# Eight taps of a 31-tap depthwise convolution as fp32 diagonal products on TensorE, in two stages of a two-block network

## The chip, the cores and the metric

The kernel runs on one core of a Trainium2 chip. The metric is the device time of one execution in microseconds (us). A core has five engines that run their own queues in order: TensorE (PE, with its weight loads listed as PEld), VectorE (DVE), ScalarE (ACT), GpSimd (POOL) and SyncE (SP), which here issues the transfers.

## The reference, cut to what matters

Two networks of two layers each run one after the other over 256 tokens of 1024 features. Each layer of the first one has a convolution branch and a recurrence branch, over `x` and over a context `ctx`:

```python
def conformer_conv(u, conv_w, conv_b, cnorm_g, cnorm_b):
    val, gate = jnp.split(u, 2, axis=-1)
    z = val * jax.nn.sigmoid(gate)
    z = dwconv(z, conv_w) + conv_b          # 31 taps per channel, 512 channels
    z = group_norm(z, CONV_GROUPS, cnorm_g, cnorm_b, LN_EPS)
    return jax.nn.silu(z)
...
    yc, s_f, s_b = rwkv_scans(prep_c, s_zero, s_zero, emit=not last)
    yx, _, _ = rwkv_scans(prep_x, s_f, s_b, emit=True)
    mix_x = jnp.concatenate([conformer_conv(ux[..., :CONV_IN], *cv), rwkv_out(yx, prep_x, *post)], axis=-1)
    x = x + gt1 * (mix_x @ w_out[l])
```

All data are fp32. The convolution output at token t is the sum over 31 taps j of `w[j, channel] * z[t + j - 15, channel]`, plus a bias per channel.

## The kernel before

Activations are kept feature-major: 128 channels on the partitions, 256 tokens along the free axis, so 512 convolution channels are four slices f = 0 to 3 of 128 x 256. Large products are made from a high and a low part of each operand (`mm3`, three products); each weight tile of 128 x 1024 (512 KB) is loaded through SP into one of four `raw` slots (L345 to L349) and split on ACT (L341) and DVE (L342).

The program is written in an order of priority, and a planner that simulates the engines (`schedule_with_timeline_sim`) turns it into one in-order queue per engine: of the instructions that it believes ready, the one written earlier goes first, and later ones fill the gaps.

The first network runs four recurrences: context and x of layer 0, context and x of layer 1. The first (`wide(0, ...)`) and the last (`wide(1, ...)`) have a convolution beside them and are the ones touched. In such a stage:

- `rwkv` prepares keys and decays, then `inverse` (L943) inverts 32 x 32 triangles by forward substitution on DVE: 31 steps of a product (L961) and a subtraction (L963), each waiting for the one before. Meanwhile PE runs `reads` (L1013 to L1038) and `values` (L1040 to L1072), whose results DVE masks (L1028, L1064). After it, `chain` (L1074) runs four steps for each of two groups.
- `filler` (L1426) hands out steps between the chain's steps in program order: first `conv_in` (L659), which makes `z` in the tile `x` (four steps, products with `in_wc`, gate on ACT at L669, product on DVE at L670), then `ada_steps` (L478): 32 weight tiles `in_ada`, each read straight from its `raw` slot by two fp32 products of 512 columns; each group of four tiles is copied by ACT (L497) and added to a bias by DVE (L503).
- `conv` (L700), written after the recurrence, makes the 31 taps of each slice. DVE multiplies the middle tap with the bias added (L718) and adds 18 taps with one instruction each (L725) into a tile `T1c`. POOL zeroes its own sum (L719), takes the 12 outer taps, each as a product (L731) and an addition (L732), and adds DVE's sum (L736). The group norm over the result follows (L744 to L762). Its instructions can run as soon as `z` is there, so the planner puts them into the recurrence as fillers.

A third convolution (over x of layer 0, `hold=True`, all 31 taps on POOL) lies beside later work. PSUM tiles of the fillers are two buffers with the tag `pb`, shared by `conv_in` and `ada_steps`.

Of the kernel before, what the change touches and what calls it, by code (L numbers as in the profile page):

```python
# [11 lines left out]
AF = mybir.ActivationFunctionType  # L12
ALU = mybir.AluOpType

P = 128
D = 1024
NF = 8
T = 256
# [16 lines left out]

NLAST = 2, 4

NPOOL, NPOOLE, NPOOLC = (12, 0), (12, 0), (30, 0)
NTAP = 2

QB, QE, QC, EVERY = (2, 3, 4, 5), (2, 3, 4, 5), (1,), 2
# [126 lines left out]
def _layout(a):  # L168
    f = {}
    n = {k: np.asarray(v) for k, v in a.items()}  # L170
# [38 lines left out]
    for l in range(2):  # L209
        f[f"ada{l}"] = n["ada_w"][l].reshape(4, 2, P, 12, 512).transpose(3, 0, 2, 1, 4).reshape(48, P, 1024)  # L210
        w = n["w_in"][l]
# [5 lines left out]
        uc = _up(w[:, :D])  # L217
        f[f"wc{l}"] = (np.stack([uc[:4], uc[4:]], 1).reshape(8, P, D))
        f[f"wo{l}"] = (n["w_out"][l].reshape(NF, P, D))
        lo = np.zeros((P, 2, 1024), np.float32)  # L220
        lo[:64, 0] = n["decay_up"][l].transpose(1, 0, 2).reshape(64, 1024)
        lo[64, 0] = n["decay_b0"][l].reshape(1024)
# [13 lines left out]
        w = n["w_in_2"][l]  # L236
# [17 lines left out]
    "A h 5,P l 5,A h 6,A h 7,D l 6,D l 7").split(",")]  # L254
EVAC = [(e, op, int(f)) for e, op, f in EVAC]
EVAC1 = [x for f in range(8) for x in (("DA"[f // 2 % 2 == 0], "e", f), ("A", "h", f), ("P" if f in (4, 5) else "D", "l", f))]


class Prog:
# [437 lines left out]
            self.split(src, *mix[f])  # L697
        return mix

    def conv(self, l, z, acc, npool, hold=False):  # L700


        nc = self.nc
        o = COLS[f"convw{l}"][0]
        taps = sorted((j for j in range(31) if j != 15), key=lambda j: abs(j - 15))
        nv, na = 30 - npool[0] - npool[1], npool[1]
        parts = [("v", taps[:nv]), ("a", taps[nv : nv + na]), ("p", taps[nv + na :])]

        order = []
        for k, js in parts:  # L710
            order += [((i + 0.5) / len(js), k, j) for i, j in enumerate(js)]
        order.sort()
        zc = [acc[:, f, :] for f in range(4)]
        for f in range(4):
            w = lambda j: self.cols[:, o + 4 * j + f : o + 4 * j + f + 1]
            av = self.T1([P, T]) if nv else None
            if nv:
                nc.vector.tensor_scalar(av, z[:, f, :], w(15), self.col(f"convb{l}", f), ALU.mult, ALU.add)  # L718
                nc.gpsimd.memset(zc[f], 0.0)  # L719
            else:  # L720
                nc.gpsimd.tensor_scalar(zc[f], z[:, f, :], w(15), None, ALU.mult)
            for i, (_, k, j) in enumerate(order):
                d, s = slice(max(0, 15 - j), min(T, T + 15 - j)), slice(max(0, j - 15), min(T, T + j - 15))
                if k == "v":
                    nc.vector.scalar_tensor_tensor(av[:, d], z[:, f, s], w(j), av[:, d], ALU.mult, ALU.add)  # L725
                else:
                    t = self.t(self.pool, [P, T], "tap", bufs=NTAP)
                    if k == "a":
                        nc.scalar.mul(t[:, d], z[:, f, s], w(j))
                    else:  # L730
                        nc.gpsimd.tensor_scalar(t[:, d], z[:, f, s], w(j), None, ALU.mult)  # L731
                    nc.gpsimd.tensor_add(zc[f][:, d], zc[f][:, d], t[:, d])  # L732
                if i % 5 == 4:
                    yield
            if nv:
                nc.gpsimd.tensor_add(zc[f], zc[f], av)  # L736
            else:
                nc.gpsimd.tensor_scalar(zc[f], zc[f], self.col(f"convb{l}", f), None, ALU.add)
# [672 lines left out]
    def first(self):  # L1411
        nc = self.nc
# [3 lines left out]
        drain = lambda g: [None for _ in g]  # L1416
# [4 lines left out]
        fl = lambda t: t.rearrange("p (a b) -> p a b", a=4)  # L1421
        z = lambda: self.t(self.pool, [P, 4, T], "z", bufs=2)

        def wide(l, x, s0, ada, perm, before=None):

            def filler():  # L1426

                steps = itertools.chain(self.conv_in(l, x, fl(self.x[0])), self.ada_steps(l, ada))

                def fill(n=1):  # L1430
                    lane = self.lane
                    self.on("b")
# [32 lines left out]
        zx = z()  # L1465
# [9 lines left out]
        f = self.out(0, self.x, 1, cm)  # L1475
# [3 lines left out]
        self.on("b")  # L1479
        acc = z()  # L1480
        self.go = False
        self.bg = self.conv(0, zx, acc, NPOOLC, True)
# [13 lines left out]
        f = self.out(0, self.x, 0, xm)  # L1496
# [141 lines left out]
```

## Time and profile before

| what | value |
|---|---|
| three timed runs | 2770.84, 2770.74, 2761.48 us (median 2770.74) |
| the profiled execution | 2761.92 us, its span 2760.1 us |
| PE busy | 2615.7 us (95% of the span) |
| DVE busy | 1724.0 us (62%) |
| ACT busy | 1312.7 us (48%) |
| POOL busy | 636.7 us (23%) |
| mean granted TensorE clock | 0.964 |

Busy time is the union of an engine's instruction times. The granted clock is a share of full speed: 1.00 is 2.4 GHz, 0.50 is 1.2 GHz, and a value between them is a mean over a stretch. Times within the execution count from the start of the span. Each fp32 product of PE appears as two records.

### The profile page before, as it was taken

To read this page: it belongs to the slowest core of one execution; us is meant where nothing else is said; L and a number is where in the kernel's file an instruction comes from. 1 tells how busy PE (TensorE), PEld (TensorE's weight loads), DVE (VectorE), ACT (ScalarE), POOL (GpSimd) and SP (SyncE) were. 2 spreads that over 40 slices of the span, in tenths; PEclk is the share of its full clock that TensorE was granted. 3 is DMA by queue.
4 is the path that set the end of the run, shared out by engine and by line. 5 is a ranking of instruction groups with operands and counts; after the bars stand their busy time and mean duration, and the time that the engine had idled before them with its cause. 6 is when DMAs were issued, how large, how long until landed. Compare 5 with 4: busy or idle time off the path is not lost.

```text
span 2760.1 us, 53694 instructions
## 1 busy us (share of the span) xinstructions
PE 2615.7 (95%) x22398; PEld 2279.0 (83%) x22398; DVE 1724.0 (62%) x2739; ACT 1312.7 (48%) x1985; POOL 636.7 (23%) x625
## 2 busy tenths in 40 slices
PE   7889989999889998889899899999999999999998
PEld 4858867888678897856799899889899898889897
DVE  3895778645577555995555655666655655756655
ACT  5514654434564346423544544644544544644543
POOL 0397999900130001384100000010000000100000
PEclk9998999999899999998999999999999999999999
DMA  7363425334323354252455555524555554425653
GB/s 252 108 207 130 144 80 187 126 129 163 114 77 116 130 183 145 100 202 93 145 184 186 195 185 188 190 77 160 184 186 182 190 184 175 164 85 183 209 187 115
DMA packets 118768, 430.71 MB, mean 156 GB/s; under 512 B 13174, under 2 KB 13686, under 8 KB 118524
## 3 DMA queue, kind: packets, MB, share of 16 engines
q1 hardware_dynamic: 118524, 427.28, 44.9%
q8 instruction: 175, 2.87, 0.4%
q14 instruction: 69, 0.57, 0.1%
HBM read 425.13 MB, written 2.10 MB: 155 GB/s over the span
## 4 chain that ended last, share of the span: by engine, by line
PE 80%; DVE 11%; ACT 4%; issue 2%; DMA 2%; POOL 1%; SPq 0%; ACTq 0%; DVEq 0%; POOLq 0%
PE pb L333 33%; PE acc L333 25%; PE ps L333 20%; DVE wl L342 3%; DVE T1c L725 1%; DVE S L963 1%; DMA raw<-in_ada 1%; DVE T L961 1%; ACT wh L341 1%; PE acc L438 1%; DVE acc L619 0%; DVE x L620 0%; DMA raw<-in_wr 0%; DVE S L849 0%; ACT L384 0%
## 5 line engine op out<-in xcount | busy, mean ns | idle before, releaser
L342 DVE TENSOR_TENSOR wl<-raw,wh 128x1024 fp32r<-128x1024 f32 (+1 forms) x654 | 811.8, 1245 | 608.6 <-ACT wh L341 383.8
L341 ACT CAST wh<-raw 128x1024 fp32r<-128x1024 f32 (+1 forms) x654 | 682.0, 1046 | 887.9 <-PE pb L333 349.7
L333 PE MATMUL pb<-xf,wh 128*128 128x256 f32 (+1 forms) x2560 | 489.2, 289 | 14.6 <-DVE T1b L588 5.1
L333 PE MATMUL pb<-S,wh 128*128 128x256 f32 x2560 | 490.5, 288 | 3.5 <-DVE S L630 1.7
L333 PEld LDWEIGHTS pb<-xf,wh 128*128 128x128 f32 (+1 forms) x2560 | 411.3, 195 | 29.2 <-DVE T1b L588 8.9
L333 PEld LDWEIGHTS pb<-S,wh 128*128 128x128 f32 x2560 | 407.0, 191 | 20.3 <-issue 11.2
L333 PE MATMUL ps<-S,wh 128*128 128x256 f32 x2048 | 390.0, 287 | 1.3 <-ACT S L460 0.9
L333 PE MATMUL pb<-xf,wl 128*128 128x256 f32 (+1 forms) x1280 | 372.0, 291 | 9.2 <-DVE wl L342 9.2
L365 POOL TENSOR_TENSOR wl<-raw,wh 128x1024 fp32r<-128x1024 f32 x22 | 52.7, 2407 | 1400.8 <-ACT wh L364 964.9
L333 PE MATMUL pb<-S,wl 128*128 128x256 f32 x1280 | 366.5, 286 | 1.8 <-DVE wl L342 1.8
L333 PEld LDWEIGHTS ps<-S,wh 128*128 128x128 f32 x2048 | 325.9, 191 | 11.2 <-issue 4.0
L333 PE MATMUL ps<-S,wl 128*128 128x256 f32 x1024 | 292.9, 286 | 0.0
L333 PEld LDWEIGHTS pb<-xf,wl 128*128 128x128 f32 (+1 forms) x1280 | 249.1, 195 | 17.1 <-DVE wl L342 12.0
L333 PEld LDWEIGHTS pb<-S,wl 128*128 128x128 f32 x1280 | 245.0, 191 | 5.2 <-issue 2.3
L333 PE MATMUL acc<-wh,T 128*128 128x512 f32 x704 | 206.3, 393 | 0.0
L333 PEld LDWEIGHTS ps<-S,wl 128*128 128x128 f32 x1024 | 195.8, 191 | 2.5 <-issue 1.5
L333 PE MATMUL acc<-wh,T1b 128*128 128x512 f32 x528 | 158.3, 398 | 3.5 <-ACT T1b L341 3.5
L731 POOL TENSOR_SCALAR tap<-z,cols 128x255 f32<-128x255 f32 (+14 forms) x120 | 148.3, 1245 | 0.0
L333 PEld LDWEIGHTS acc<-wh,T 128*128 128x128 f32 x704 | 127.0, 189 | 23.6
L731 POOL TENSOR_SCALAR tap<-x,cols 128x246 f32<-128x246 f32 (+5 forms) x96 | 110.7, 1163 | 46.1 <-DVE x L670 46.1
L333 PEld LDWEIGHTS acc<-wh,T1b 128*128 128x128 f32 x528 | 95.2, 190 | 22.4 <-ACT T1b L341 4.4
L333 PE MATMUL acc<-wl,T 128*128 128x512 f32 x352 | 113.1, 395 | 0.0
(444 smaller groups left out, 3907.6 us busy)
## 6 DMA issues: line engine op xcount, KB each, us to landing
raw<-in_fu SPq DMA_DIRECT2D x132, 512.0 KB, 3.2
raw<-in_ada SPq DMA_DIRECT2D x96, 512.0 KB, 4.2
raw<-in_pu SPq DMA_DIRECT2D x88, 512.0 KB, 4.2
raw<-in_qu SPq DMA_DIRECT2D x88, 512.0 KB, 3.3
raw<-in_fd SPq DMA_DIRECT2D x66, 512.0 KB, 3.2
raw<-in_wr SPq DMA_DIRECT2D x51, 512.0 KB, 3.5
raw<-in_pd SPq DMA_DIRECT2D x44, 512.0 KB, 4.0
raw<-in_qd SPq DMA_DIRECT2D x44, 512.0 KB, 3.3
```

The lines of the kernel that those rows point to most:

```text
L333: return self.nc.tensor.matmul(out, lhsT, rhs, start=start, stop=stop, **kw)
L341: self.nc.scalar.copy(hi, src)
L342: self.nc.vector.tensor_sub(lo, src, hi.bitcast(F32))
L365: self.nc.gpsimd.tensor_sub(lo, r, hi.bitcast(F32))
L438: nc.tensor.transpose(pt[f // 2][:, f % 2, b, :], yb[b][:, f * P : f * P + P], self.cst("ident"))
L725: nc.vector.scalar_tensor_tensor(av[:, d], z[:, f, s], w(j), av[:, d], ALU.mult, ALU.add)
L731: nc.gpsimd.tensor_scalar(t[:, d], z[:, f, s], w(j), None, ALU.mult)
L961: nc.vector.tensor_mul(tv, tj[:, k + 1 : 32, k : k + 1].broadcast_to([P, m, k + 1]), X[:, k : k + 1, 0 : k + 1].broadcast_to([P, m, k + 1]))
L963: nc.vector.tensor_sub(X[:, k + 1 : 32, 0 : k + 1], X[:, k + 1 : 32, 0 : k + 1], tv)
```

## The change

A new step `conv_first` makes the eight middle taps (15, 14, 16, 13, 17, 12, 18, 11) of each slice on PE: for each tap an fp32 product of a 128 x 128 diagonal matrix with the shifted slice of `z`, all eight summed in one PSUM tile. ACT copies the sum to `acc` and adds the bias. The diagonals are made on the host (`cd0`, `cd1`: four tiles of 512 KB for each layer) and loaded through the same `raw` slots. `conv_first` stands in the filler between `conv_in` and `ada_steps`. In `conv`, DVE zeroes its sum with a memset and adds 12 taps, and POOL takes 11 taps and adds them to the `acc` that ACT wrote. The held convolution keeps its 31 taps on POOL, with the bias now in its first instruction.

```diff
-NPOOL, NPOOLE, NPOOLC = (12, 0), (12, 0), (30, 0)
+TAPS = sorted(range(31), key=lambda j: abs(j - 15))
+NTENS, NPOOL = 8, 11
...
+    def conv_first(self, l, z, acc):
+        for f in range(4):
+            r = self.raw(f"cd{l}", f)
+            pc = self.ps((P, T))
+            for i, j in enumerate(TAPS[:NTENS]):
+                d, s = tap(j)
+                self.mm(pc[:, d], r[:, i * P : i * P + P], z[:, f, s], i == 0, i == NTENS - 1)
+            self.nc.scalar.activation(acc[:, f, :], pc, AF.Identity, bias=self.col(f"convb{l}", f))
+            yield
...
-                nc.vector.tensor_scalar(av, z[:, f, :], w(15), self.col(f"convb{l}", f), ALU.mult, ALU.add)
-                nc.gpsimd.memset(zc[f], 0.0)
+                av = self.T1([P, T])
+                nc.vector.memset(av, 0.0)
+                for j in TAPS[NTENS : 31 - n]:
+                    d, s = tap(j)
                     nc.vector.scalar_tensor_tensor(av[:, d], z[:, f, s], w(j), av[:, d], ALU.mult, ALU.add)
...
-                steps = itertools.chain(self.conv_in(l, x, fl(self.x[0])), self.ada_steps(l, ada))
+                steps = itertools.chain(self.conv_in(l, x, fl(self.x[0])),
+                                        self.conv_first(l, fl(self.x[0]), fl(self.x[1])), self.ada_steps(l, ada))
...
-            drain(self.conv(l, fl(self.x[0]), fl(self.x[1]), (NPOOL, NPOOLE)[l]))
+            drain(self.conv(l, fl(self.x[0]), fl(self.x[1])))
```

## Rows read from the trace of the kernel before

**Rows 1.** Page, engines: busy time, share of the span, instructions of PE.

```profile
PE 2615.7 (95%) x22398; PEld 2279.0 (83%) x22398; DVE 1724.0 (62%) x2739; ACT 1312.7 (48%) x1985; POOL 636.7 (23%) x625
```

**Rows 2.** Chain that ended last, shares by line, in four stretches (139-163, 163-206, 1160-1197, 1197-1262).

```profile
by line: DVE T1c L725 49.6%; DVE wl L342 16.3%; DVE T L961 9.6%; DVE S L963 6.7%; DVE S L1028 6.5%; issue 4.5%; DVE x L670 2.8%; PE acc L333 2.7%; DVE T1c L718 2.7%
...
by line: PE pb L333 52.3%; PE acc L333 21.5%; DMA raw<-in_ada 15.2%; PE acc L1051 4.9%; PE acc L1034 3.8%; ACT T2b L497 2.8%; issue 0.6%; ACTq L497 0.1%
...
by line: DVE T1c L725 41.7%; DVE wl L342 17.0%; DVE S L963 11.5%; DVE T L961 9.7%; DVE S L1028 7.7%; DVE T1c L718 4.9%; DVE x L670 3.6%; issue 3.0%; PE acc L1034 1.3%
...
by line: PE pb L333 45.2%; PE acc L333 30.4%; DMA raw<-in_wo 9.9%; PE ps L333 7.3%; PE acc L1051 3.2%; ACT T2b L497 2.7%; PE acc L1034 2.6%; issue 0.5%; ACTq L497 0.1%
```

**Rows 3.** Busy by stretch, first stage: PE, PEld, DVE, ACT, POOL; clock, DMA, GB/s.

```profile
130.00:206.00 76.00, 67.10 (x657) 44.22 (x660) 73.39 (x156) 16.76 (x29) 68.69 (x65) 0.93 0.57 196
206.00:230.00 24.00, 24.00 (x393) 16.80 (x392) 12.30 (x22) 10.15 (x14) 23.51 (x29) 0.64 0.47 173
230.00:300.00 70.00, 69.03 (x852) 56.31 (x851) 41.80 (x79) 34.22 (x59) 48.20 (x52) 1.00 0.30 101
```

**Rows 4.** Busy by stretch, last stage, the same columns.

```profile
1160.00:1233.00 73.00, 63.96 (x633) 42.32 (x635) 72.03 (x153) 15.18 (x27) 63.32 (x63) 0.95 0.56 196
1233.00:1262.00 29.00, 28.63 (x549) 21.77 (x548) 16.45 (x30) 12.78 (x19) 28.37 (x35) 0.82 0.52 176
```

**Rows 5.** The first row of rows 3 in two parts, the same columns.

```profile
139.00:163.00 24.00, 17.15 (x192) 14.21 (x192) 24.00 (x44) 3.47 (x6) 23.61 (x23) 0.93 0.28 98
163.00:206.00 43.00, 41.26 (x380) 21.73 (x378) 40.39 (x97) 9.83 (x18) 37.53 (x36) 0.92 0.78 267
```

**Rows 6.** DVE by line, 130 to 206: busy us, mean ns, idle before.

```profile
L725 DVE SCALAR_TENSOR_TENSOR T1c<-x,cols,T1c 128x254 f32<-128x254 f32 (+8 forms) x72 | 42.1, 618 | 0.0
...
L718 DVE TENSOR_SCALAR T1c<-x,cols 128x256 f32<-128x256 f32 x4 | 1.8, 440 | 0.0
```

**Rows 7.** Line 725 over the whole span: durations min/median/max in ns.

```profile
L725 DVE SCALAR_TENSOR_TENSOR T1c<-x,cols,T1c x144: 456/476/960, 132.9 to 1230.9; 128x255 f32<-128x255 f32 x16, 128x254 f32<-128x254 f32 x16, 128x253 f32<-128x253 f32 x16, 128x252 f32<-128x252 f32 x16
```

**Rows 8.** PE in order of time (start, us): two successive fp32 products of 256 columns.

```profile
1289.80 0.60 PE L333 MATMUL acc<-x,const 128*128 128x256 f32 x2
1290.23 0.59 PE L333 MATMUL acc<-rks,const 128*128 128x256 f32 x2
```

**Rows 9.** Other groups of that shape over the span: busy us, mean ns of a record.

```profile
L333 PE MATMUL ps<-wa,S 128*128 128x256 f32 x40 | 10.6, 403 | 0.0
...
L333 PE MATMUL ps<-z,const 128*128 128x256 f32 x8 | 4.9, 715 | 0.5 <-DVE z L751 0.5
```

**Rows 10.** PE in order of time, instructions before which it waited.

```profile
141.25 0.39 PE L333 MATMUL pb<-xf,wl 128*128 128x256 f32 x1 [1.37 <-DVE wl L342]
...
153.61 0.38 PE L333 MATMUL pb<-xf,wl 128*128 128x256 f32 x1 [1.98 <-DVE wl L342]
```

**Rows 11.** SP in order of time: issues of loads in the first stage.

```profile
135.94 79.76 SPq L348 DMA_DIRECT2D raw<-in_ada  x32
224.67 8.21 SPq L348 DMA_DIRECT2D raw<-in_wc  x6
```

**Rows 12.** POOL in order of time: its first and last convolution work.

```profile
131.30 1.89 POOL L731 TENSOR_SCALAR tap<-x,cols 128x246 f32<-128x246 f32 x2 [23.33 <-DVE x L670]
...
1265.44 0.78 POOL L736 TENSOR_TENSOR x<-x,T1c 128x256 f32<-128x256 f32 x1
```

**Rows 13.** POOL by line, 130 to 206: busy us, mean ns, idle before.

```profile
L731 POOL TENSOR_SCALAR tap<-x,cols 128x246 f32<-128x246 f32 (+5 forms) x32 | 41.0, 1291 | 23.3 <-DVE x L670 23.3
L732 POOL TENSOR_TENSOR x<-x,tap 128x246 f32<-128x246 f32 (+5 forms) x31 | 26.1, 841 | 1.1
```

**Rows 14.** DVE in order of time: first reader of the finished convolution, last stage.

```profile
1288.69 0.42 DVE L751 TENSOR_TENSOR x<-x,acc 128x256 f32<-128x256 f32 x1 [0.87 <-PE acc L333]
```

**Rows 15.** ACT in order of time: an eviction of 128x256 from PSUM.

```profile
128.82 0.38 ACT L669 ACTIVATE T1b<-pb 128x256 f32<-128x256 f32 x1
```

More of the change, by code (lines that the diff above doesn't have):

```diff
@@ L219, in _layout @@
         f[f"wo{l}"] = (n["w_out"][l].reshape(NF, P, D))
+        cw, cd = n["conv_w"][l].reshape(31, 4, P), np.zeros((4, P, NTENS, P), np.float32)
+        for i in range(NTENS):
+            for p in range(4):
+                cd[p, np.arange(P), i, np.arange(P)] = cw[TAPS[i], p]
+        f[f"cd{l}"] = cd.reshape(4, P, NTENS * P)
         lo = np.zeros((P, 2, 1024), np.float32)
@@ L256, with tap @@
 EVAC1 = [x for f in range(8) for x in (("DA"[f // 2 % 2 == 0], "e", f), ("A", "h", f), ("P" if f in (4, 5) else "D", "l", f))]
+def tap(j):
+    return slice(max(0, 15 - j), min(T, T + 15 - j)), slice(max(0, j - 15), min(T, T + j - 15))
 class Prog:
@@ L698, in mixed_in, with conv @@
         return mix
-    def conv(self, l, z, acc, npool, hold=False):
+    def conv_first(self, l, z, acc):
[7 more added lines that the diff above has]
+            yield
+    def conv(self, l, z, acc, hold=False):
         nc = self.nc
         o = COLS[f"convw{l}"][0]
[L705 to L712, printed above, removed]
+        n = 31 if hold else NPOOL
         zc = [acc[:, f, :] for f in range(4)]
@@ L715, in conv @@
             w = lambda j: self.cols[:, o + 4 * j + f : o + 4 * j + f + 1]
-            av = self.T1([P, T]) if nv else None
-            if nv:
-                nc.vector.tensor_scalar(av, z[:, f, :], w(15), self.col(f"convb{l}", f), ALU.mult, ALU.add)
-                nc.gpsimd.memset(zc[f], 0.0)
-            else:
[L721 to L724, printed above, removed]
+            if hold:
+                nc.gpsimd.tensor_scalar(zc[f], z[:, f, :], w(15), self.col(f"convb{l}", f), ALU.mult, ALU.add)
+            else:
+                av = self.T1([P, T])
+                nc.vector.memset(av, 0.0)
+                for j in TAPS[NTENS : 31 - n]:
+                    d, s = tap(j)
                     nc.vector.scalar_tensor_tensor(av[:, d], z[:, f, s], w(j), av[:, d], ALU.mult, ALU.add)
[L726 to L732, printed above, removed]
+            for i, j in enumerate(TAPS[1:] if hold else TAPS[31 - n :]):
+                d, s = tap(j)
+                t = self.t(self.pool, [P, T], "tap", bufs=NTAP)
+                nc.gpsimd.tensor_scalar(t[:, d], z[:, f, s], w(j), None, ALU.mult)
+                nc.gpsimd.tensor_add(zc[f][:, d], zc[f][:, d], t[:, d])
                 if i % 5 == 4:
                     yield
-            if nv:
+            if not hold:
                 nc.gpsimd.tensor_add(zc[f], zc[f], av)
-            else:
-                nc.gpsimd.tensor_scalar(zc[f], zc[f], self.col(f"convb{l}", f), None, ALU.add)
             yield
@@ L1481, in first @@
         self.go = False
-        self.bg = self.conv(0, zx, acc, NPOOLC, True)
+        self.bg = self.conv(0, zx, acc, True)
         self.mods, self.every = self.ada_steps(1, QC), EVERY
```

## Prediction

> **What bounds the kernel now.** I read the page's engine totals first: PE is busy for 2615.7 us of 2760.1 [rows 1], so 144.4 us of PE idle time is all that the kernel has, anywhere. Work taken from another engine is worth only what it lets PE stop waiting; work given to PE costs its full length except where it lands in that idle time, or lets PE run at its higher clock for longer.
>
> Then I read the chain that ended last, in the two stages that are edited. Each has two parts. Early in the inversion the chain lies on DVE: from 139 to 163 the taps of L725 hold 49.6% of it (11.9 us), and from 1160 to 1197 41.7% (15.4 us) [rows 2]. Later, from 163 to 206 and from 1197 to 1262, it lies on PE: the pb and acc products are 74% and 76% of it, and no tap stands on it [rows 2]. So the taps are costly in the first part and free in the second.
>
> Third, the busy time by stretch. From 130 to 206 DVE is busy 73.39 of 76.00 us, but PE also 67.10, at a mean clock of 0.93 [rows 3]. So PE is idle for 8.9 us. Of that 6.85 lie between 139 and 163 and 1.74 between 163 and 206 [rows 5]. In the last stage PE is idle for 9.04 us of the 73 from 1160 to 1233 [rows 4]. After the inversion PE has no room left: 24.00 of 24.00 and 69.03 of 70.00 in the first stage [rows 3], 28.63 of 29.00 in the last [rows 4].
>
> The clock is a second reserve. It has two levels, 1.2 and 2.4 GHz. A mean of 0.93 over 76 us means 10.6 us at the lower one, and half of that, 5.3 us, is what it cost [rows 3]. In the last stage 0.95 over 73 us gives 7.3 us and 3.7 us [rows 4]. The fall comes where PE has waited for DVE: 1.37 us at 141 and 1.98 us at 153 [rows 10].
>
> **The change part by part.**
>
> *Products added to PE.* Each stage gets 4 slices x 8 taps = 32 fp32 products, of 252 to 256 columns. Successive products of this shape start 0.43 us apart (1289.80 and 1290.23 [rows 8]). 32 x 0.43 = 13.8 us a stage, 27.5 us for both. The upper bound for the usual clock is the product of `ps<-wa,S`: 40 records are 20 products in 10.6 us, 0.53 us each [rows 9], 17 us a stage. At the low clock it would be 1.22 us (8 records, 4 products, 4.9 us [rows 9]), 39 us if all 32 met it. I take 0.43, because these are back to back in one PSUM tile like the pair of rows 8.
>
> *What of this PE would have idled through.* A product of slice f can start when z[f] is there (the first at 131.3, when POOL starts on it [rows 12]), when its diagonals have landed, and when one of two pb buffers is free. The loads queue on SP behind those of `in_wc`, in the place where the 32 of `in_ada` begin at 135.94 [rows 11]. So from about 140 on some products can lie in the 6.85 us of idle time between 139 and 163. Bounds: 0 (if the planner's simulation sees no gap there, or the buffers are held by `conv_in`) and all 8.9 us. I take 5.0 us, a little over half, since the idle time is in the right place and the buffers only partly.
>
> *Clock.* If PE waits less before 160, part of the 5.3 and 3.7 us comes back. Bounds 0 and 5.3; I take 1.5 us a stage, since the small 32 x 32 products and the remaining waits stay as they are.
>
> *Taps removed from DVE.* Six of 18 per slice, 24 a stage, at 42.1 us / 72 = 0.585 us each [rows 6]: 14.0 us. The middle tap of L718 (0.44 us [rows 6]) becomes a memset of the same size, which I put between 0 and that price. DVE falls from 73.4 to about 59 us in the stretch and ceases to be the fuller engine. The instructions of L725 take 476 ns in the median and up to 960 [rows 7]; the long ones lie where POOL works on taps too. The Trainium skill ("SBUF — State Buffer", section "SBUF: two separate sides") says that a DVE instruction with two SBUF inputs and a GpSimd instruction that reads SBUF lock each other out for a whole instruction. By that rule the taps removed should be counted at the free price, 24 x 0.476 = 11.4 us, and the remainder is waiting that other DVE work would inherit. Either way this relief is no term of the sum: it is the means by which PE's idle time shrinks, counted above.
>
> *POOL.* One tap of 12 per slice goes: 4 x (1.291 + 0.841) = 8.5 us less [rows 13], and four memsets. But its additions now wait for the first eviction of PE's sum instead of a memset done long before. In the last stage POOL ends at 1266.2 [rows 12] and the first reader of the finished slice, the group norm, comes at 1288.69 [rows 14]: 22 us of cover. A later start of 15 us less 8.5 us of work stays under it: 0. The cover is gone once the start is over 31 us late, and each further microsecond would then count.
>
> *ACT.* Four evictions a stage at 0.38 us [rows 15], 1.5 us, on an engine that is busy for 16.76 us of 76 [rows 3]: 0.
>
> *Transfers.* Four loads of 512 KB a stage, ahead of the 32 of `in_ada` on SP and in the same four slots. The 32 take 79.76 us, 2.5 us each [rows 11], so four in turn would push the `in_ada` stream by 10 us. Between 139 and 163 the transfers fill only 0.28 of the DMA engines' time, from 163 to 206 0.78 [rows 5], so the loads themselves find room; the push is the slots held until z[f] exists. In the first stage the next loads, `in_wc` at 224.67, come right behind the stream [rows 11] and PE needs them soon after. I take 0, because PE then has its own 13.8 us of work in place of `in_ada`'s, and keep 10 us as the upper bound for the first stage. In the last stage nothing is late.
>
> *The held convolution* loses four POOL instructions of at most 1.3 us [rows 13] out of a POOL run that PE does not wait for in the edited stages: 0.
>
> *Sum.* Per stage 13.8 - 5.0 - 1.5 = +7.3 us; two stages +14.6. Some of the first half of the stage may run earlier because DVE's queue is shorter, so I round down to +13. Against the profiled execution, 2761.9 us, that is 2775. The timed runs show two values, 2761.5 and twice 2770.8; the profiled one is at the lower, the median, 2770.7, at the upper. On the median the forecast is 2784 us.
>
> **The rivals.**
>
> *No change: PE's reserves take it all.* Idle 8.9 + 9.0 and clock 5.3 + 3.7 are 26.9 us, against 27.5 of new work. For it: with DVE relieved, the waits for wl in rows 10 should nearly vanish. Against: the planner fills every gap that it sees on DVE with taps as long as there are any, so the early part stays dense until they run out. Time: -8 to +4 us, 2763 to 2775.
>
> *Faster: the inversion is the true end and PE's fill moves behind it.* DVE's 24 taps less, 14 us a stage, bring the inversion's end from 206 towards 192, and the filler products of `in_ada` that are still to do run in the stretch after it, where PE's clock is 0.64 [rows 3] because it only runs small products. If dense work kept the clock up there, up to 24 x 0.36 = 8.6 us would come back in the first stage and 29 x 0.18 = 5.2 us in the last [rows 3, 4]. The Trainium skill ("TensorE: Matmul & The Clock Gate", section "Part 1: The HAM clock gate (the "warmup" mystery)") has the clock follow how busy the array has been, which speaks for it. With that and all of the idle time the change comes to 27.5 - 26.9 - 13.8 = -13 us, and down to -20 if the shorter DVE queue also brings later waits down. It decides from the point where PE, with its new products but with part of the filler left for later, reaches the inversion's end in the 59 us that DVE then needs. Time: 2750 to 2757.
>
> *Much slower: a late end.* The `in_ada` stream is pushed by its 10 us in the first stage with PE waiting for `in_wc`, or POOL ends past its cover, or the products run at 0.53 us or partly at the low clock (+6 to +15). Time: +25 to +40 us, 2796 to 2811. For it: the two pb buffers are held by `conv_in` nearly throughout the early part, which would put all 32 products behind 163, where PE has 1.74 us of room [rows 5].
>
> *That the change does not do what it says*: the planner could leave the taps on the chain as dense as now. That is the upper half of the forecast.
>
> **How the numbers follow.** Forecast (+4 to +24 us): 0.52. No change: 0.16. Faster: 0.18. Late end: 0.14. A change of 0.5% (13.9 us) is about what a measurement of this kernel can tell from none. Half of the forecast lies above that: slower 0.26 + 0.14 = 0.40; within 0.5% 0.26 + 0.16 = 0.42; faster 0.18. The range must hold 0.8: the forecast and no change are 0.68; I add most of the late end, up to +33 us, and the nearer end of the faster case, down to -17 us: 2754 to 2804. The forecast's own range is 2775 to 2795.
>
> **What would show it.** Right: 64 products with `in_cd` at about 0.43 us, PE busy up by 24 to 30 us, its idle time between 139 and 163 (and 1160 to 1197) down by several us, L725 at 96 records, and the chain that ended last on PE instead of L725. DVE then has idle time late in the inversion. Wrong in the sum: PE's busy time rising by much less than 27 us, which would be the clock; or the whole of the last stage ending earlier than now. Wrong in the cover: POOL's last addition after the group norm's other centring steps, or PE waiting on `in_wc` loads after the first stage.

## The result, and the profile after

The changed kernel takes 2807.04 us (median of five runs, 2803.8 to 2814.22) against 2770.74 us for the kernel before beside it: ratio 1.0145, 95% interval 1.0124 to 1.0165. It is slower, by 36 us between the medians. The forecast was 2784 us with a range up to 2804. Runs more than 1.5% above the fastest of the same kernel are left out of all comparisons below; there is one, in an experiment.

The profiled execution took 2804.08 us, its span is 2802.3, 42.2 longer than that of before. The engine line of its page, to be read against [rows 1]:

```profile
PE 2657.2 (95%) x22526; PEld 2319.7 (83%) x22526; DVE 1699.3 (61%) x2691; ACT 1317.8 (47%) x1996; POOL 585.0 (21%) x597
```

PE has 41.5 us more busy time and 128 more records, DVE has 24.7 us less, POOL 51.7 us less. PE is idle for 145.1 us, against 144.4: none of its idle time was saved in sum.

Where the time came in is read from the two stages. A fixed piece of work bounds each: from SP's first load of `in_wc` to the first of `in_fu` behind it for the first stage, from the first load of the last context's `in_wr` to the `in_fu` behind it for the last. The busy time by stretch (PE, PEld, DVE, ACT, POOL; granted clock, DMA share, GB/s), before:

```profile
94.29:358.78 264.49, 249.00 (x2879) 198.09 (x2869) 198.49 (x381) 118.16 (x204) 200.60 (x207) 0.94 0.45 155
1046.45:1322.14 275.69, 245.96 (x2913) 187.84 (x2912) 207.01 (x395) 117.44 (x204) 128.17 (x138) 0.93 0.38 131
```

and after:

```profile
96.35:387.80 291.45, 270.27 (x2945) 219.19 (x2935) 183.95 (x353) 125.13 (x212) 168.35 (x190) 0.89 0.42 148
1074.83:1364.38 289.55, 266.63 (x2975) 208.65 (x2974) 191.41 (x370) 117.97 (x208) 105.98 (x126) 0.91 0.38 132
```

The first stage is 27.0 us longer, the last 13.9. Each length can be split into three: PE idle (length less busy time), clock loss (one minus the granted clock, times the length: what the stretch would be shorter at full clock, if all of it went by the clock), and the rest, which is called work at full clock. Added over ten equal parts of each stage, since the clock has only two digits, this gives for the change: first stage idle +5.7, clock loss +15.8, work +5.5; last stage idle -6.8, clock loss +8.8, work +11.9. The split is good to some 6 us (a stage in which nothing is changed shows shifts of that size between its parts, below). It puts too much into the clock loss: the products alone are 14.5 us a stage (below), and the work term shows +5.5 and +11.9. A group of eight 64 x 64 records takes 0.68 us at 1.00 (187.89 in the kernel before) and 1.11 at 0.50 (210.74 in the changed one), 1.6 times and not twice. The lengths are no better than some 6 us either: two stages in which nothing is changed moved by 0.7 and 2.1, two kernels with the same first stage took 282.6 and 276.9 us for it, and the 688 us between the two stages, where only the held convolution's bias is changed, are 8.4 us shorter to 12.0 longer than before in the fifteen profiles.

The first stage in finer stretches, for [rows 3] and [rows 5]:

```profile
139.00:163.00 24.00, 24.00 (x274) 22.14 (x273) 24.00 (x57) 5.17 (x9) 4.55 (x5) 1.00 0.32 110
163.00:206.00 43.00, 33.42 (x349) 24.35 (x348) 31.26 (x58) 9.91 (x15) 42.06 (x52) 0.65 0.29 98
206.00:230.00 24.00, 24.00 (x353) 17.08 (x352) 6.04 (x15) 7.02 (x15) 23.53 (x31) 0.70 0.30 106
230.00:300.00 70.00, 67.04 (x769) 45.12 (x767) 28.47 (x62) 24.07 (x46) 8.11 (x11) 0.95 0.60 213
```

From 139 to 163 PE no longer idles at all, where it idled 6.85 us. From 163 to 206 it idles 9.6 us instead of 1.7, and its clock is 0.65 instead of 0.92. Transfers fill 0.29 of the DMA engines' time there instead of 0.78: the stream of `in_ada` stands still. PE in order of time around 176, with the wait ahead of an instruction in brackets:

```profile
172.14 0.68 PE L345 MATMUL acc<-S,S 64*64 64x64 f32 x8
172.75 1.06 PE L345 MATMUL pb<-raw,csil 128*32 128x512 f32 x6
180.65 1.60 PE L345 MATMUL acc<-S,S 64*64 64x64 f32 x16 [6.84 <-DVE T L1074]
```

and DVE, which it waited for (L971 and L973 are the inversion's steps, L739 the taps):

```profile
175.60 0.67 DVE L739 SCALAR_TENSOR_TENSOR T1c<-x,cols,T1c 128x246 f32<-128x246 f32 x1
...
179.59 0.40 DVE L971 TENSOR_TENSOR T<-S,S 128x87 f32<-128x87 f32 x1
180.02 0.25 DVE L973 TENSOR_TENSOR S<-S,T 128x87 f32<-128x87 f32 x1
180.18 0.41 DVE L1074 TENSOR_TENSOR T<-acc,const 64x256 f32<-64x256 f32 x1
...
181.38 0.58 DVE L973 TENSOR_TENSOR S<-S,T 128x31 f32<-128x31 f32 x1
```

The inversion on DVE ends at 182.0, where before it ended at 204.5. But the mask product T of `values`, on which the next PE instruction waits, has been queued behind almost all of it. Behind that wait PE is at 0.50 until about 220. Up to 188.5 it runs four products of `in_ada` there, and from then to 218 none, but mostly 64 x 64 and 32 x 32 products. SP's issues in the first stage, for [rows 11]:

```profile
137.77 13.09 SPq L360 DMA_DIRECT2D raw<-in_cd  x4
157.74 80.55 SPq L360 DMA_DIRECT2D raw<-in_ada  x20
...
240.35 20.18 SPq L360 DMA_DIRECT2D raw<-in_ada  x12
264.06 5.87 SPq L360 DMA_DIRECT2D raw<-in_wc  x5
```

`in_ada` begins 21.8 us later, and `in_wc` 39.4 us later. In PE's queue only 10 of the 64 products of `in_ada` now stand ahead of the inversion's last product, in either stage; before it was 56.

The products themselves, and the taps left, over the span:

```profile
L345 PE MATMUL pb<-x,raw 128*128 128x255 f32 (+4 forms) x128 | 29.0, 380 | 0.0
...
L739 DVE SCALAR_TENSOR_TENSOR T1c<-x,cols,T1c x96: 459/472/925, 134.2 to 1225.0; 128x251 f32<-128x251 f32 x16, 128x250 f32<-128x250 f32 x16, 128x249 f32<-128x249 f32 x16, 128x248 f32<-128x248 f32 x16
```

128 records are 64 products in 29.0 us of busy time, 0.45 us each.

The last stage begins 28.4 us later than before (1074.83 against 1046.45). Its first row below, for [rows 4], ends with PE at 0.96, and the 57 us behind it are at 0.60:

```profile
1160.00:1233.00 73.00, 64.87 (x740) 57.24 (x738) 70.00 (x151) 24.03 (x42) 30.36 (x35) 0.96 0.37 131
1233.00:1290.00 57.00, 55.22 (x811) 44.30 (x810) 23.43 (x48) 15.31 (x26) 47.82 (x61) 0.60 0.17 58
```

In the kernel before, the same part of the stage, 28.4 us earlier, was at 0.91:

```profile
1204.62:1261.62 57.00, 55.76 (x820) 35.82 (x820) 43.48 (x93) 18.30 (x28) 53.11 (x59) 0.91 0.64 221
```

### The profile page after: what moved, and what is told of

It reads as the page before. It is cut to its first block, busy times and chain, and to the rows that moved or that the text cites. A ratio compares the mean times of both kernels' runs of the same rounds, so it can differ in the third digit from the quotient of the medians.

```text
span 2802.3 us, 53922 instructions
## 1 busy us (share of the span) xinstructions
PE 2657.2 (95%) x22526; PEld 2319.7 (83%) x22526; DVE 1699.3 (61%) x2691; ACT 1317.8 (47%) x1996; POOL 585.0 (21%) x597
## 4 chain that ended last, share of the span: by engine, by line
PE 79%; DVE 12%; ACT 4%; DMA 2%; issue 2%; POOL 1%; SPq 0%; DVEq 0%; ACTq 0%; POOLq 0%
PE pb L345 32%; PE acc L345 26%; PE ps L345 20%; DVE wl L354 2%; DVE T1c L739 2%; DMA raw<-in_ada 1%; DVE T L971 1%; DVE S L973 1%; ACT wh L353 1%; PE acc L450 1%; POOL tap L743 0%; DVE S L860 0%; DVE tDb L531 0%; DVE acc L631 0%; ACT L396 0%
## 5 line engine op out<-in xcount | busy, mean ns | idle before, releaser
L345 PEld LDWEIGHTS acc<-wh,T1b 128*128 128x128 f32 x528 | 95.8, 191 | 23.5 <-ACT T1b L353 4.4
L744 POOL TENSOR_TENSOR z<-z,tap 128x255 f32<-128x255 f32 (+14 forms) x120 | 105.3, 878 | 4.0
```

The costliest lines, as they stand in the source:

```text
L345: return self.nc.tensor.matmul(out, lhsT, rhs, start=start, stop=stop, **kw)
```

## The experiments

Each difference is between medians of runs on one chip, with the 95% interval of the ratio; different rows can come from different chips. "First" and "last" are the lengths of the two stages against before in the profiled execution, bounded as above; they do not add up to the difference, which is of other runs and has the time outside the stages in it.

| kernel | against before, us | ratio | first | last |
|---|---|---|---|---|
| changed kernel | +36.3 | 1.0124-1.0165 | +27.0 | +13.9 |
| in_ada held back, nothing else | +49.6 | 1.0167-1.0193 | +29.1 | +25.2 |
| taps out, no products | +14.1 | 1.0041-1.0069 | +2.2 | +14.4 |
| products beside all taps | +43.0 | 1.0141-1.0168 | +29.5 | +25.6 |
| the same, products late | +23.5 | 1.0072-1.0104 | +17.4 | +15.4 |
| in_ada urgent | +45.4 | 1.0152-1.0184 | +24.7 | +20.8 |
| no loads | +30.7 | 1.0094-1.0128 | +12.5 | +18.8 |
| in_ada urgent, no loads | +40.3 | 1.0104-1.0178 | +29.6 | +29.1 |
| T first | +37.6 | 1.0121-1.0155 | +25.6 | +18.3 |
| T first, in_ada urgent | +44.6 | 1.0138-1.0185 | +31.5 | +8.5 |
| T first, in_ada urgent, no loads | +18.5 | 1.0043-1.0079 | +11.6 | +14.9 |
| VectorE keeps 18 taps | +33.6 | 1.0099-1.0140 | +26.0 | +20.1 |
| products behind in_ada | +56.3 | 1.0183-1.0221 | +18.1 | +46.3 |
| the same, first stage only | +10.1 | 1.0030-1.0063 | +12.4 | -2.1 |
| last stage only | +13.5 | 1.0035-1.0064 | -0.7 | +19.6 |

**Is the displaced filler enough by itself?** The kernel before, with PE's products of `in_ada` held behind the inversion:

```diff
-self.conv_in(l, x, fl(self.x[0])), self.ada_steps(l, ada)
+self.conv_in(l, x, fl(self.x[0])), self.held(3, self.ada_steps(l, ada))
...
+with self.tc.issue_after(self.lastinv.ins) if i >= n else contextlib.nullcontext():
```

> The kernel before, all taps on VectorE and GpSimd, no diagonals. One edit: in both stages the products with in_ada from the fourth step on are ordered on TensorE behind the last 32 x 32 product of the inversion, so 12 of 64 run before it instead of 56 (10 in the changed kernel). Theory D (the displaced in_ada products cost what the sum did not hold: TensorE then has only small products during the inversion, at 1.2 GHz and with waits): +10 to +20 us against before, mean granted clock down from 0.964 to about 0.958. Theory W (the unexplained 14 us belong to the diagonal products or their loads themselves): 0, within 4 us.

Measured +49.6 us, with no work added: more than the whole change costs, and two and a half times the top of what the theory allowed. PE idles 15.2 us more in the first stage and 10.3 in the last, and the clock loss rises by 15.5 and 21.9. The loads of `in_ada` wait as well, since its products hold the slots (0.05 of the DMA engines' time from 173 to 206). So the order of the filler is a term of the size of the result. The share that I had given it, in proportion to 14 us, was far too small.

**Fewer taps alone, and products alone.** In the first, `conv_first` is taken out of the changed kernel; in the second, it is added to the kernel before.

```diff
-self.conv_first(l, fl(self.x[0]), fl(self.x[1])), self.ada_steps(l, ada)
+self.ada_steps(l, ada)
```

> The changed kernel without the diagonal products, their loads and their evictions: the eight middle taps and the bias of the two convolutions are left out of the computation, so what is timed is the relief of VectorE and GpSimd alone. 40 and 32 of the 64 products of in_ada run before the inversion's end (56 before). The prediction's own steps (10 us of idle time and 3 us of clock come back): -13 us against before. Theory D: relief and displacement nearly cancel, -6 to +6 us. Theory W (TensorE never gains from fewer taps, nothing is lost either): 0, within 3 us.

```diff
-self.conv_in(l, x, fl(self.x[0])), self.ada_steps(l, ada)
+self.conv_in(l, x, fl(self.x[0])), self.conv_first(l, fl(self.x[0]), None), self.ada_steps(l, ada)
```

> The kernel before with all its taps, and in addition the 64 diagonal products, their loads and evictions (to a tile that nothing reads): the added work alone. 24 and 32 of the 64 products of in_ada run before the inversion's end (56 before). The prediction's product term: +27.5 us, less what lands in idle time, so +18 to +28. Theory D: 27.5 plus 32 + 24 of the 92 displaced products at 14.5 us for all, +33 to +40. Theory W: the products carry the whole loss, +42 within 4 us.

Relief alone costs 14.1 us where the prediction's steps gave -13 us and theory D allowed +6 at most: nearly all of it in the last stage, where 32 of 64 products of `in_ada` are left ahead of the inversion's end, and it is clock loss there (+15.8). That the missing 24 products are the cause is argued from this, not shown. Products alone cost 43.0 us. That is theory W's number (42 within 4) and above theory D's, and within the intervals as much as the whole change: by the medians the relief pays back 6.7 us.

**Is it the products, or where they stand?** The products beside all taps, ordered behind the inversion's last product:

```diff
-self.conv_first(l, fl(self.x[0]), None), self.ada_steps(l, ada)
+self.ada_steps(l, ada), self.held(0, self.conv_first(l, fl(self.x[0]), None))
```

> The kernel before with all its taps, and the 64 diagonal products, their loads and evictions in addition (evicted to a tile that nothing reads), as in the run with the products beside all taps; one edit more: the products are traced after the steps of in_ada and ordered on TensorE behind the last 32 x 32 product of the inversion, so 56 of 64 products of in_ada run before the inversion's end, as before. Theory P (it is the place of the products, ahead of in_ada's and of the value products, that costs the 15 us beyond their own 27.5): +14 to +30 us against before, with the stretch up to the inversion's end as before, and less than 27.5 where the products lift the clock behind the inversion. Theory W (the 15 us belong to the products wherever they stand): +38 to +46.

Measured +23.5: 19.5 us less than the same products ahead of `in_ada`, and less than their own length (64 x 0.45 = 28.8 us, by the rows above). In the first stage the clock loss is that of before (+0.1) and the work +14.6. This settles that the loss beyond the products' own length belongs to their place, on PE and, with their loads, on SP. The last stage still has +10.4 of clock loss there, which stays unexplained.

**Putting the filler back.** In the changed kernel the steps of `in_ada` get a higher priority.

```diff
-self.ada_steps(l, ada)
+self.at(-1000, self.ada_steps(l, ada))
```

> The changed kernel with one edit: the steps of in_ada get a higher priority in the planner, so that 40 (first stage) and 56 (last stage) of their 64 products run before the inversion ends, instead of 10 and 10; taps, diagonals and their loads as changed. Theory D: the time falls by 8 to 15 us against the changed kernel, to +27 to +34 us against before; the last stage, where all 56 are back, gives back most of its half. Theory W: as the changed kernel, +42 within 5 us.

Measured +45.4: a miss for theory D. It is theory W's number (42 within 5), but the run above with the products late speaks against its cause. The filler is back in PE's queue, and the clock still falls. The stretch from 173 to 206, in the columns used above, in the kernel before:

```profile
173.00:206.00 33.00, 31.93 (x312) 17.43 (x316) 30.39 (x71) 7.14 (x14) 32.18 (x30) 0.95 0.77 261
```

in the changed kernel:

```profile
173.00:206.00 33.00, 24.18 (x295) 17.66 (x290) 21.26 (x39) 7.04 (x10) 32.30 (x42) 0.55 0.25 84
```

and in this one:

```profile
173.00:206.00 33.00, 26.54 (x252) 15.61 (x254) 18.87 (x36) 8.01 (x11) 32.29 (x41) 0.57 0.37 125
```

PE's wait for T is still there (its view of waits: us in total, times, longest), and so are the diagonals' loads ahead of `in_ada` on SP.

```profile
PE acc L352 <- DVE T L1081: 6.5, 1, 6.5
```

**Without the loads.** The identity in SBUF takes the diagonals' place in the changed kernel, first alone, then with the filler urgent as well.

```diff
-r = self.raw(f"cd{l}", f)
+r = self.cst("ident")
```

> The changed kernel without the eight loads of diagonals: the stationary operand of all 64 products is the identity that is in SBUF already, so the weights of the eight middle taps are left out of the computation. Planner's order of in_ada 10 and 14 of 64 before the inversion's end. Theory P (order on TensorE): as the changed kernel, +35 to +45 us against before. Theory L (the loads hold the four slots and SyncE's queue ahead of in_ada's, which starts 20 us late): in_ada's first load back near 136 us and +20 to +30.

> The changed kernel with both suspects of the first stage taken away: no loads of diagonals (the identity stands in their place, so the weights of the eight middle taps are left out of the computation) and the steps of in_ada at a higher priority in the planner. 56 and 48 of the 64 products of in_ada run before the inversion's end (56 and 56 before). Theory P + L (order on TensorE and the place of the loads on SyncE are the whole of the first stage's loss beyond the products): the first stage costs 11 to 16 us instead of 26, of which half clock at most 4; the whole +22 to +34 us against before. If a third cause is in the first stage (the wait on VectorE's T alone lets the clock fall for 35 us): the first stage stays at 20 or more, the whole at +38 or more.

Without loads: +30.7, between the two theories. `in_ada` starts at 137.6 us, and the first stage costs 12.5 us instead of 27.0, so about half of that stage's cost comes with the loads; the last stage gains nothing (+18.8), and the whole only 5.6 us by the medians. What goes is not the fall of the clock from 173 to 206, which is as deep as in the changed kernel, behind a wait of 6.0 us for T and with the same 10 products of `in_ada` ahead:

```profile
173.00:206.00 33.00, 27.00 (x382) 21.21 (x375) 23.02 (x41) 9.86 (x15) 32.29 (x40) 0.59 0.22 77
```

It is what follows: the clock is at 1.00 from 215 to the end of the stage, where the changed kernel is at 0.50 until 220 and falls again between 270 and 280 and between 330 and 340. The clock loss is +4.0 instead of +15.8, the idle time -1.6 instead of +5.7, the work +10.1 instead of +5.5.

With the filler urgent as well: +40.3, in five runs spread from 2785 to 2824 us, the profiled one the slowest. In that execution the third cause is there: PE waits 7.0 us for T, and the clock from 173 to 206 is 0.53.

**Taking the wait for T away.** In the changed kernel the inversion's last seven steps are ordered behind the first T on DVE:

```diff
-nc.vector.tensor_mul(tv, ...)
-nc.vector.tensor_sub(X[...], X[...], tv)
+with self.tc.issue_after(self.firstT.ins) if k0 is not None and k >= k0 else contextlib.nullcontext():
+    nc.vector.tensor_mul(tv, ...)
+    nc.vector.tensor_sub(X[...], X[...], tv)
```

> The changed kernel with one edit on VectorE: the last seven steps of the inversion's elimination are ordered behind the first two mask products T of the value products, on which TensorE waited 6.8 us with its clock falling to 1.2 GHz for the next 40 us. TensorE's order stays nearly that of the changed kernel (16 instead of 10 products of in_ada ahead of the inversion's end), and so do the diagonals, their loads and all work. Theory S (that one wait lets the clock fall, and the small products behind it keep it low): the wait falls under 2 us, the clock stays at 2.4 GHz for most of 173 to 206, and the first stage costs 12 to 18 us instead of 26; the whole +22 to +34 us against before. Theory O (the order of TensorE's work alone does it, with small products and no in_ada between): the wait goes, but the clock still falls before 190 us and the first stage stays at 22 or more; the whole +36 to +46.

The longest wait for T falls to 2.2 us, and the time is +37.6 us: theory S falls, and the time lies in theory O's range. The clock holds longer, but is at 0.50 from 188 on, in a stretch without a product of `in_ada` (183.5 to 221). It falls in the second of two waits, of 1.7 and 2.2 us, so the run does not tell the missing products from the waits. Then both edits together, with and without the loads:

> The changed kernel with both edits that failed alone: the last seven elimination steps of the inversion stand behind the first mask products T on VectorE, and the steps of in_ada have a higher priority, so that 54 and 60 of their 64 products run before the inversion's end (56 and 56 before). Theory C (both conditions are needed: no long wait, and in_ada's products between the small ones): the mean clock from 173 to 206 is 0.9 or more, the first stage costs 11 to 18 us instead of 26, the whole +24 to +34 us against before. Theory N (neither matters; the clock falls for a reason not named yet): the clock in that stretch stays at 0.7 or less, the first stage at 22 or more, the whole +38 to +48.

> The same without the eight loads of diagonals (the identity in their place, so the weights of the eight middle taps are left out of the computation): 48 and 52 of 64 products of in_ada before the inversion's end, and in_ada's first load at its old time. Theory C with the loads as a third part: 4 to 10 us less than the run with the loads, because in_ada's stream starts 20 us earlier. Theory C alone: within 4 us of it.

From 173 to 206, with T first alone:

```profile
173.00:206.00 33.00, 27.21 (x366) 20.25 (x368) 21.91 (x41) 9.76 (x14) 32.37 (x40) 0.67 0.33 117
```

with both edits, there and in the next stretch:

```profile
173.00:206.00 33.00, 32.16 (x387) 18.05 (x385) 22.10 (x44) 10.94 (x16) 32.37 (x40) 0.99 0.75 251
...
203.00:251.00 48.00, 48.00 (x341) 25.62 (x342) 5.13 (x14) 6.49 (x12) 21.17 (x28) 0.53 0.43 145
```

and with both edits and no loads:

```profile
173.00:206.00 33.00, 31.55 (x340) 17.39 (x338) 22.59 (x42) 11.24 (x17) 32.29 (x41) 0.90 0.73 254
...
203.00:251.00 48.00, 48.00 (x614) 28.92 (x613) 12.24 (x27) 13.60 (x25) 29.73 (x39) 0.82 0.62 215
```

In that stretch theory C holds: of the kernels that keep the products ahead of `in_ada`, only those with both edits have the clock up, at 0.99 and 0.90. In the total it holds only without the loads, and the loads are worth 26.1 us between the two medians, where 4 to 10 were expected. With them the clock falls from 203 to 251 instead, which costs 48 x (0.82 - 0.53) = 13.9 us more than in the other run. Without them the first stage ends at +11.6, made of work +17.2, idle -6.2 and clock loss +0.7: with the order, the wait and the loads all out of the way, products and recovered idle time come out near the prediction's 13.8 and -5.0. The run with the loads is one execution of 2819.6 us, the slowest of five (2799.9 to 2819.6), so this picture is that of its bad case, and 12.0 of its 57.7 us lie between the two stages.

Both clocks fall alike, with PE busy throughout, behind 32 x 32 products followed by products of two columns (60 and 8 records from 201.63, 73 and 8 from 203.18). What PE runs next differs. Without the loads it is twelve records of `in_ada` together, and the clock is at 1.00 again from 214 to 216, though not for good; with them it is groups of four, once eight, with small products between, to 251:

```profile
207.89 3.62 PE L352 MATMUL pb<-raw,csil 128*32 128x512 f32 x12
...
207.55 1.92 PE L352 MATMUL pb<-raw,csil 128*32 128x512 f32 x4
```

No run separates this from the later stream of loads.

**Whose relief, which order, which stage.** VectorE with all 18 taps and GpSimd with 5; the products traced behind `in_ada`; that in the first stage only; the change in the last stage only. (In the last two, the other stage has its convolution of before.)

```diff
-NTENS, NPOOL = 8, 11
+NTENS, NPOOL = 8, 5
```

> The changed kernel with VectorE keeping all 18 of its taps a slice, and GpSimd down from 11 to 5: the relief goes to GpSimd alone. 30 and 28 of 64 products of in_ada run before the inversion's end. If the relief of VectorE is worth anything to TensorE, this is slower than the changed kernel by up to 10 us. Theory P (relief is worth nothing, order is all): between the changed kernel and the one with the products late, +32 to +40 us against before.

```diff
-self.conv_first(l, fl(self.x[0]), fl(self.x[1])), self.ada_steps(l, ada)
+self.ada_steps(l, ada), self.conv_first(l, fl(self.x[0]), fl(self.x[1]))
```

> The changed kernel with one edit: the diagonal products are traced after the steps of in_ada instead of ahead of them. 40 of the 64 products of in_ada run before the inversion's end in either stage (10 in the changed kernel, 56 before). Theory P: 27.5 of work, and 16 of 46 displaced products' share of the rest in each stage: +28 to +36 us against before. Against it stands the late end: GpSimd's additions then begin only behind the products, and if the group norm of the last stage waits for them the time is +40 or more.

> The change in the first stage only, with the diagonal products traced behind the steps of in_ada; the last stage as before. 40 of 64 products of in_ada run before the inversion's end in the first stage, 56 in the last, as before. The same first stage cost 10.6 us in the run with both stages so ordered. Theory P: +8 to +16 us against before, that is, the 13.8 us of products less some 3, and nothing in the last stage. If the change can win anywhere, it is here; no theory expects less than +5.

> The change in the last stage only, the first stage as before. 56 of 64 products of in_ada run before the inversion's end in the first stage, 6 in the last. If the two stages add up: +10 to +18 us against before (the last stage of the changed kernel cost 13.9), and the first stage's loads at their old times within 2 us. If the last stage's cost depends on what the first left behind: over +22 or under +6.

With 24 more taps a stage on VectorE the kernel is not slower than the changed one (+33.6 against +36.3, intervals overlapping). No gain from VectorE's relief shows, but 30 and 28 products of `in_ada` stand ahead of the inversion's end here instead of 10, so the run does not separate relief and order; and its profile, for the stage columns, is the slowest of five (2817.8 us, median 2801.6). With the products behind `in_ada` the time is the worst of all, +56.3, and all of the excess is in the last stage, where GpSimd's sums now start too late:

```profile
PE acc L345 <- POOL x L748: 34.1, 3, 15.6
```

That is the late end which the prediction's GpSimd step had bounded by 22 us of cover; it came true in this kernel, not in the changed one. In the first stage alone the same order costs 10.1 us, the cheapest form of the change found; that stage has 6.8 us less clock loss than before, and its clock from 173 to 206 is 0.87. (The 10.6 us in its expectation were counted to the first load of `in_wo`, which this order moves; to the bound of the table it is 18.1 in the one run and 12.4 in the other.) The change in the last stage alone costs 13.5 us, as expected if the stages add up. Its last stage is 19.6 us longer in the profile, against 13.9 in the changed kernel, in another order of PE's queue (6 and 10 products of `in_ada` ahead of the inversion's end). Its first stage, where nothing is changed, is 0.7 us off in length and 3.2 off in clock loss; the last stage of the run before it, also as before, is 2.1 off in length and up to 6.4 in its parts: that is how far the split can be trusted, at best.

No version was faster than the kernel before.

## Why the prediction was wrong, step by step

*Products added to PE: right.* 0.43 us each was forecast, 29.0 us of busy records over 64 products make 0.45, and the other 12.5 of the 41.5 us by which PE's busy time rose are put down to the lower clock.

*Idle time recovered, -5.0 a stage: right where it was looked for, wrong in the sum.* Between 139 and 163 PE's 6.85 us of idle time went to zero, more than forecast, and the last stage kept a gain of 6.8. It did not go quite as the step had it: the diagonal products begin only at 154.02, and before that it is `conv_in`'s products that no longer wait for `wl`. Taps out alone leaves 6.6 us idle there, products alone 6.0. In the first stage the next stretch gave back 7.8 us, most of it one wait of 6.84 us for T. The step asked which gaps the products would fill, and not whose place in PE's in-order queue they would take: they stand ahead of the value products, and T stands behind nearly all of the inversion's steps on DVE. PE came to the wait at 173.8, DVE to T at 180.18; that the planner believed the two closer is argued from this, not shown.

*Clock, -1.5 a stage: the step that failed.* It measured +15.8 and +8.8, by a split that puts somewhat too much into this term. The prediction read the clock as a reserve of 5.3 and 3.7 us that could only come back [rows 3, 4]. The same rows held the warning: 206 to 230 has PE busy for 24.00 of 24.00 us at 0.64, and there it runs, without a wait,

```profile
206.88 1.98 PE L333 MATMUL ps<-S,S 32*32 32x32 f32 x64
208.68 4.32 PE L333 MATMUL acc<-S,S 32*32 32x32 f32 x80
```

with the clock at 1.00 until 208 and at 0.50 from 209 on. So small products alone did not hold the clock. From 163 to 206, at 0.92, `in_ada` products stand among them, and the step did not ask what the change does to these. Held back alone, they cost 49.6 us, though with 15.2 and 10.3 us more of waiting. The step also misread where the clock falls: behind the wait of 1.37 us at 141 it stays at 1.00, to 151; it is at 0.50 from 154 to 157, behind the one of 1.98, and falls again by 164 and 175, the second time with no wait over 0.74 us ahead of it.

*Transfers, taken at 0 with 10 us as the bound: mis-sized.* `in_ada` began 21.8 us later, not 10: the loads of the diagonals hold the four slots until the products run, from 154.02, and its first load is issued at 157.74. In the first stage this is worth 14.5 us (27.0 against 12.5 without the loads), and 19.9 us in the pair with both other causes removed (31.5 against 11.6, the former from the longest of five runs). In the last stage it is worth nothing, as forecast. It is no third term to add to the others: of the 14.5 us, 11.8 are clock loss and 7.3 idle time, with 4.6 of work the other way.

*Taps removed from DVE, no term of their own: right as a sum, not as the means.* The relief alone saves no idle time (+1.1 and +2.7 us) and costs 14.1 us in all; that it does so by way of the filler's order is argued.

*POOL, ACT, the held convolution: right.* POOL's last sum ended at 1282.0 and nothing waited for it, though in the first stage its additions waited 22.1 us for ACT's first eviction, not 15.

*The rivals.* The faster case described what happened, the inversion ending early (182.0 instead of 204.5, by more than the 14 us forecast) with `in_ada` behind it, and had the sign of it wrong: it expected the displaced dense products to lift the clock behind the inversion, and did not price the stretch that they left. (Nor does PE only run small products from 206 to 230: 7.4 of the 24 us are `in_ada`'s.) Beside it stood a rule of the Trainium skill, "TensorE: Matmul & The Clock Gate", section "Part 1: The HAM clock gate (the "warmup" mystery)", that the clock follows how busy the array has been. The runs agree so far: where the dense products were taken out, the clock fell (0.55 from 173 to 206 in the changed kernel and 0.60 with in_ada held, against 0.95). The late end was the nearest in time (+25 to +40) and named the push of `in_ada`, but at 10 us and with PE waiting for `in_wc`, which the trace doesn't show.

**What stays open.** Two things are shown: with small products alone the clock falls without any wait (206.88 in the kernel before), and with `in_ada` among them it falls, and stays low for 35 us and more, if PE has waited 6.5 to 7.0 us (in_ada urgent, with and without the loads). In the runs with in_ada held and with T first, waits of 1.6 us and more stand beside the missing products, so these do not show either by itself. Why the clock stays low from 203 to 251 with the loads and comes back without, with PE busy for 48.00 of 48.00 us in both, is not settled: the stream of `in_ada`, some 19 us later, and the groups in which its products stand differ together. Nor is it settled how much of the first stage's loss is the place of the products on PE and how much that of their loads: without the loads it nearly goes, with the order and the wait as they were, and with in_ada urgent and no loads it is back, in the longest of the five runs counted. Nor is it settled why the last stage, in the same orders, moves by less: its cost lies between 8.5 and 20.8 us in the forms of the change that keep the products ahead of `in_ada` and have the loads, and one profile of each is too few to rank them.

## What to carry to other kernels

Where PE is the bound and a planner fills its waits, price an edit by what it does to the order of the filler, not only by the work it adds and removes: read which dense products keep the clock up in the stretch, and check in the new queue order whether they are still there. New work ahead of old filler displaces it twice, on the engine and in the queue of its loads. Here the relief of an engine that was busy for 97% of a stretch brought no gain that a run could show; the engine beside it was busy for 88% of it, and its filler was displaced by the same edit.

## What the runs showed of the hardware

The granted clock can stay at 1.2 GHz for 40 us and more while the profile shows PE busy without a gap: 48.00 of 48.00 us at 0.53 in the rows above, with 52 records of 512-column products among the small ones at 1037 ns each. By line, that run from 203 to 251 (busy us, mean ns):

```profile
L352 PE MATMUL pb<-raw,csil 128*32 128x512 f32 x52 | 22.5, 1037 | 0.0
```

and the kernel before from 173 to 206, at 0.95, where the same records took 641 ns:

```profile
L333 PE MATMUL pb<-raw,csil 128*32 128x512 f32 x68 | 16.5, 641 | 0.7 <-DMA raw<-in_ada 0.7
```

The Trainium skill, "TensorE: Matmul & The Clock Gate", section "HAM oscillation — how this bites in real kernels", tells of a clock that falls when PE waits between bursts of products. That agrees with the fall behind the 6.84 us wait. The fall at 205 in the run above, and the one at 208 in the kernel before, come with PE waiting for nothing.

GpSimd's tap products took 966 ns in the mean from 130 to 206, against 1291 ns before [rows 13], with DVE's taps down from 72 to 48 in that stage; DVE's own took 565 ns in the mean against 618 [rows 6]. DVE's are longer where both engines are at work on taps: in the changed kernel 514 ns from 139 to 163, where POOL is busy for 4.55 of 24 us, and 688 ns from 163 to 206, where it is busy for 42.06 of 43.

```profile
L743 POOL TENSOR_SCALAR tap<-x,cols 128x245 f32<-128x245 f32 (+5 forms) x28 | 26.8, 966 | 24.1 <-DVE x L682 24.1
```

The same program can differ from run to run by 1.4%: the one with `in_ada` urgent and no loads took 2785 to 2824 us in five runs, with a mean granted clock from 0.972 in the fastest to 0.955 in the slowest, where the kernel before stayed within 0.5% (2759.97 to 2774.45) at 0.959 to 0.966.
